# A weight gradient by seven products: two sums in other places, three stores in halves, and a new hand-written order

## The chip, the cores and the metric

The kernel runs on one core of a Trainium2 chip, in one launch. TensorE (PE) multiplies into PSUM, which has eight banks of 128 x 512 float32; VectorE (DVE) and ScalarE (ACT) empty and fill the banks and do sums; GpSimd (POOL) here only issues the loads, SyncE (SP) and ACT issue a few loads and the stores. The engines run apart from each other and wait for each other's semaphores. The metric is the device time of one execution in microseconds, as the median of several runs.

## The reference

```python
def reference(input: np.ndarray, grad_output: np.ndarray) -> np.ndarray:
    grad_weight = np.einsum('bmk,bmn->kn', input, grad_output)
    return grad_weight.astype(np.float32)
```

`input` is 16 x 512 x 1024 and `grad_output` 16 x 512 x 768, both float32. The result is one 1024 x 768 matrix: a product with a contraction over all 8192 rows.

## The kernel before

The rows are loaded 256 at a time, in 32 loads of each input (`LOADS`). Seven of the loads ("s") are taken as two single tiles of 128 rows each, 14 in all, whose products are the plain ones. The other 25 ("P") are pairs of tiles, on which a scheme with seven products in place of eight is used. The loads convert float32 to bfloat16 on the way, except for the very first tiles, which are loaded as float32 and rounded by DVE and ACT (L201).

The output is cut into four quarters: A (left columns, first half of the rows), B (right, first), C (left, second) and D (right, second), each of four blocks of 128 x 384, q = 0 to 3. For pairs seven products are summed over all items: A, B and C go on in the sums of the quarters, and 1, 5, 6 and 7 have sums of their own (`macc`; `SLOT` says where). D gets only the plain products. That makes 14 x 4 x 4 + 25 x 7 x 4 = 924 matmuls of 384 columns. For products 5, 6 and 7 DVE forms sums of the operands: `sum_x` (L183, L185, L187) and `sum_g` (L193, L195, L197), three steps each for each pair.

All of a block's matmuls can't stay in one bank for the whole run: there are 32 sums and eight banks. So a block is opened on a bank, gets a few matmuls, and is closed; a running sum is kept in SBUF. There are two ways to go on with a sum:

- `fill` (L264): ACT copies the sum back into a bank, and the matmuls add to it; the close is then a copy out, by ACT (L321) or DVE (L323).
- fresh: the matmuls start the bank anew, and the close is an add on DVE (L325).

The order of all engines' work is written out by hand in `PLAN`, a string of tokens read from left to right, which engines then carry out in that order, each for itself: `A0@1.2` is two matmuls of block A0, opened on bank 1 (without `@`: on the bank that it has); `fA2@6` fills A2 into bank 6; `cA2` and `vA2` close it by ACT or by DVE; `g0.7`, `g1.7`, `g2.7` and `x...` are the operand sums of item 7; `r0` to `r4` are roundings of the first tiles. `fB2@1+2` fills a block in two parts, 256 columns in bank 1 and 128 in bank 2, and its matmuls are then done first for the one and then for the other.

A block's last close is always on DVE. It brings the shared sums in (`SHARED`, L310), and for product 5 makes two results:

```python
nc.vector.tensor_sub(out=dst, in0=b, in1=sum_of("6", q))                      # L306
nc.vector.tensor_sub(out=sum_of("6", q), in0=b, in1=sum_of("7", q))           # L307
```

B then adds the first of them (slot 5) and D the second (slot 6). L307 writes the slot that L306 reads, and in the built program it waits for L306 by DVE's own semaphore. After the final close of A, B, C and D the block is stored (L315), by SP, except for the part of 128 columns, which ACT stores. The stores take the eight semaphores of their kind in turn. In the built program the last but one, 128 columns on ACT's queue, has the fourth, and the 256 columns on SP's queue the fifth. At the very end SP waits for the eight of them one after the other, first to eighth, and then come the barriers of all engines.

The plan's last tokens are `52.4 vD3 vB0 C2.6 v52 fD2@0 fB2@1+2 D0.2 vC2 D2.2 B2.6 vD0 vD2 vB2`.

Of the kernel before, what the change touches and what calls it, by code (L numbers as in the profile page):

```python
# [9 lines left out]
P = 128  # L10
# [9 lines left out]


PLAN = (
    "A0@0.1 A2@1.1 A3@2.1 A1@3.1 vA2 C2@6.1 cA3 C3@7.1 C0@4.1 r0 cC2 C1@5.1 vC3 B0@1.1 B1@2.1 B2@6.1 cB0 "
    "r1 B3@7.1 r2 r3 vB1 D0@1.2 r4 A0.1 vB2 A1.1 cB3 D1@2.2 vD0 D2@6.2 cD1 D3@7.2 vD2 C0.1 C1.1 cD3 "
    "C2@1.1 C3@2.1 B0@6.2 vC2 B1@7.2 vC3 fA2@1 A0.1 A1.1 vB0 C0.1 A3@2.2 vB1 A2.2 B2@6.2 vA3 cA2 B3@7.3 "
    "vB2 C1.2 vB3 C3@2.2 C2@1.2 vC3 D0@6.2 D1@7.2 vC2 D2@2.2 vD0 fD3@1 A0.2 vD1 C0.2 fA3@6 D3.3 vD2 "
    "B2@7.2 cD3 A3.2 vB2 B1@2.2 cA3 A2@1.3 vB1 fB3@6 B0@7.3 vA2 fD2@2 B3.2 vB0 C3@1.2 cB3 D2.2 vC3 D1@7.2 "
    "cD2 C2@6.2 vD1 fD0@1 A1.3 vC2 A3@2.1 D0.2 vA3 B1@7.1 D3@6.1 cD0 C1.2 vB1 fB2@2 A0.1 C0.3 vD3 B2.3 "
    "C2@1.2 cB2 D2@7.2 vC2 A2@6.2 fC3@2 A1.2 vD2 fD1@1 C3.2 vA2 D0@7.2 cC3 D1.2 vD0 D3@6.2 cD1 A3@2.2 vD3 "
    "B1@7.2 B0@1.2 vA3 fB3@6 A0.2 vB1 C1.2 vB0 B3.4 fA2@7 A3@2.2 vB3 B0@1.2 A2.2 vA3 fB1@6 A0.2 vB0 cA2 "  # L30
    "A1.2 fB2@2 B1.2 C2@1.2 cB1 C3@7.2 vC2 C0.2 fD1@6 C1.2 vC3 fD2@1 B2.2 fD3@7 D1.4 vB2 D2.4 cD1 D3.4 "
    "cD2 D0@2.1 g0.6 D0.3 cD3 B3@6.1 g1.6 fA2@7 B3.1 vD0 C3@1.2 A2.1 g2.6 A2.1 fA3@2 A0.2 vB3 cA2 A1.2 "
    "vC3 A3.2 fC2@6 x0.6 A3.1 fB0@7 C0.3 cA3 C2.1 x1.6 C2.2 C1.1 x2.6 C1.2 cC2 B1@1.1 g0.7 B1.2 fA2@6 "
    "B0.3 vB1 B2@2.2 g1.7 cB0 B2.1 A2.1 g2.7 fC3@1 A0.1 10@7.1 vB2 A1.1 cA2 C3.1 v10 13@2.2 cC3 x0.7 "
    "12@6.2 c13 11@7.2 v12 73@1.2 c11 52@2.1 x1.7 52.1 c73 70@6.2 x2.7 53@7.2 c52 g0.8 C0.1 c70 50@1.2 "
    "v53 51@2.2 c50 g1.8 60@6.2 v51 fB3@7 A0.1 61@1.2 c60 g2.8 A1.1 B3.2 v61 C2@6.2 x0.8 cB3 C1.2 10@2.2 "
    "vC2 71@1.2 x1.8 71.1 72@7.3 v10 c71 63@6.1 x2.8 63.2 c72 g0.9 62@1.3 fB0@2 v63 C3@7.2 c62 B0.1 g1.9 "
    "B0.1 fA3@6 A1.1 vC3 C0.1 A0.1 fA2@1 g2.9 A3.2 x0.9 cB0 A3.1 A2.3 cA3 13@7.1 x1.9 f11@2 13.1 C1.1 vA2 "
    "A0.1 fB1@6 C0.1 x2.9 11.2 fB2@1 B1.3 v13 c11 g0.10 B2.3 f52@7 vB1 73@2.2 cB2 52.1 g1.10 52.1 f12@6 "
    "A1.1 v73 70@1.2 c52 12.1 g2.10 12.1 f53@2 x0.10 12.1 50@7.2 c12 53.3 v70 f61@6 C1.1 x1.10 51@1.3 c53 "  # L40
    "v50 61.2 x2.10 f60@2 61.1 C2@7.1 g0.11 C2.1 c61 60.3 v51 fB3@6 A0.1 g1.11 C0.1 62@1.2 c60 vC2 B3.2 "
    "g2.11 B3.1 C3@2.3 v62 cB3 x0.11 10@7.3 f71@1 A1.2 f72@6 vC3 71.2 x1.11 71.1 72.3 v10 c71 63@2.1 "
    "x2.11 63.2 f13@7 g0.12 B0@1.3 c72 v63 13.2 73@6.1 g1.12 fA2@2 73.1 vB0 C0.1 A0.1 c13 C1.1 g2.12 A2.2 "
    "f11@1 x0.12 A2.1 A3@7.3 cA2 v73 11.2 f52@2 x1.12 11.1 70@6.3 vA3 c11 52.1 x2.12 52.2 f50@1 g0.13 "
    "51@7.2 c52 50.3 v70 12@2.1 g1.13 12.1 c50 B1@6.3 v51 fB2@1 C1.1 g2.13 C2@7.3 v12 C0.1 x0.13 C0.1 "
    "f53@2 A1.2 B2.3 vB1 A0.1 x1.13 A0.1 cB2 53.3 vC2 f62@1 60@6.1 g0.14 60.2 c53 62.1 x2.13 62.2 g1.14 "
    "61@7.3 v60 c62 B3@2.1 g2.14 B3.2 f10@1 v61 C3@6.3 x0.14 f71@7 10.3 vB3 C1.2 c10 71.1 x1.14 71.2 vC3 "
    "73@1.3 c71 x2.14 13@2.2 f72@6 g0.15 13.1 A1.1 fB0@7 C0.1 v13 72.3 g1.15 B0.3 v73 c72 63@2.1 g2.15 "
    "63.2 cB0 x0.15 A0.2 f11@6 A2@7.3 v63 f12@1 11.2 x1.15 11.1 12.3 vA2 c11 51@2.1 x2.15 fA3@7 51.2 "
    "g0.16 B1@6.3 c12 v51 A3.2 f52@1 g1.16 A3.1 C1.1 vB1 50@2.3 cA3 g2.16 52.3 f70@6 v50 fC2@7 A1.2 x0.16 "  # L50
    "70.3 c52 C2.1 x1.16 C2.2 c70 B2@2.1 x2.16 B2.2 cC2 g0.17 53@1.3 f60@7 vB2 62@6.3 g1.17 60.3 f61@2 "
    "v53 C0.1 g2.17 C0.1 c60 61.3 v62 B3@7.1 x0.17 B3.2 f13@6 C3@1.3 c61 vB3 13.2 f72@2 x1.17 13.1 C1.2 "
    "vC3 c13 72.2 x2.17 72.1 f63@6 73@1.1 g0.18 73.2 c72 10@7.1 g1.18 10.2 fB0@2 v73 63.3 g2.18 B0.3 v10 "
    "c63 A0.1 x0.18 A0.2 cB0 C0.2 f51@7 71@1.1 x1.18 71.3 fA3@2 x2.18 A1.2 v71 A3.3 g0.19 51.3 cA3 52@6.1 "
    "g1.19 52.2 c51 g2.19 B1@1.3 v52 f11@7 A2@2.3 vB1 f12@6 11.2 x0.19 f50@1 11.2 12.4 vA2 c11 x1.19 50.3 "
    "c12 x2.19 50.1 70@2.1 fC2@6 g0.20 70.3 c50 B2@7.1 g1.20 B2.3 v70 f53@1 C2.1 g2.20 C2.2 vB2 53.3 cC2 "
    "60@2.3 v53 f62@6 C1.2 x0.20 fB3@1 C1.1 61@7.3 v60 62.2 x1.20 62.1 B3.3 v61 c62 C3@2.1 g0.21 C3.2 cB3 "
    "13@6.1 x2.20 f10@7 13.2 g1.21 A0.2 f72@1 vC3 10.3 g2.21 72.3 v13 c10 A1.1 x0.21 A1.2 c72 C0.3 fA3@1 "
    "x1.21 73@2.3 x2.21 73.1 63@6.1 g0.22 63.3 v73 B0@7.4 v63 fA2@2 A3.2 g1.22 A3.1 vB0 A2.3 cA3 g2.22 "
    "51@6.3 f71@7 vA2 C1.2 f52@1 x0.22 A0.2 f12@2 52.4 v51 x1.22 71.4 fB1@6 v52 B1.1 g0.23 B1.2 c71 12.1 "  # L60
    "x2.22 12.2 cB1 g1.23 C2@1.3 c12 g2.23 50@7.3 vC2 f13@2 11@6.2 x0.23 fB2@1 11.2 13.3 v50 B2.3 v11 c13 "
    "53@7.1 x1.23 53.2 cB2 g0.24 53.1 f60@6 70@2.4 v53 f62@1 60.1 x2.23 60.2 f61@7 g1.24 60.1 62.4 v70 "
    "c60 g2.24 C0.3 fB3@6 v62 61.2 x0.24 fC3@1 61.2 10@2.4 v61 C3.1 x1.24 f72@7 C3.3 v10 B3.2 g0.25 cC3 "
    "B3.2 fA2@2 x2.24 72.2 g1.25 72.2 cB3 A2.1 g2.25 A2.2 c72 A1.3 cA2 x0.25 A1.1 C1.3 f63@2 x1.25 A0.3 "
    "x2.25 A3@1.4 g0.26 73@6.4 vA3 51@7.2 g1.26 51.2 fB0@1 v73 63.2 g2.26 63.2 v51 B1@6.3 c63 x0.26 B1.1 "
    "fC2@7 B0.4 vB1 C2.2 x1.26 cB0 C2.2 12@2.1 x2.26 12.2 cC2 g0.27 12.1 50@6.4 f71@7 v12 52@1.1 g1.27 "
    "fB2@2 52.3 v50 71.1 g2.27 71.3 f13@6 v52 B2.2 x0.27 c71 B2.2 C0.2 cB2 x1.27 C0.1 13.2 x2.27 13.2 "
    "11@1.2 c13 g0.28 11.2 53@7.4 f60@6 v11 70@2.1 g1.28 f61@1 70.3 v53 60.1 g2.28 60.3 v70 61.2 x0.28 "
    "c60 61.2 fB3@2 A0.3 v61 A1.2 x1.28 fC3@1 A1.1 C1.2 x2.28 C1.1 62@7.1 g0.29 62.3 g1.29 62.1 B3.5 v62 "
    "g2.29 A2@6.4 vB3 C3.1 x0.29 C3.4 vA2 10@7.2 cC3 x1.29 10.3 f63@6 x2.29 72@2.5 v10 g0.30 A3@1.4 f10@7 "  # L70
    "v72 63.4 vA3 f11@2 C0.1 g1.30 C0.1 c63 13@1.1 g2.30 13.2 x0.30 f12@6 11.3 v13 12.3 c11 x1.30 12.1 "
    "f61@1 10.1 A0.2 v12 f63@2 A1.2 x2.30 c10 61.3 f62@6 63.1 C1.2 v61 f60@7 62.2 v63 fA2@1 C0.1 60.3 v62 "
    "fA3@2 A2.4 v60 f71@6 A0.2 f72@7 vA2 A1.2 71.4 vA0 f70@1 vA1 f73@0 A3.3 v71 f51@3 C1.2 vA3 73.5 vC1 "
    "51.5 v73 f53@2 fC3@5 70.3 v51 fD1@0 53.3 fB1@6 C3.3 v70 f50@3 C0.2 v53 fD3@1 B1.7 vC3 fB3@2 50.4 vC0 "
    "vB1 B3.4 v50 fD0@4 72.1 fB0@5 D1.2 D3.2 vB3 B0.7 v72 f52@3 fC2@6 vD1 52.4 vD3 vB0 C2.6 v52 fD2@0 "
    "fB2@1+2 D0.2 vC2 D2.2 B2.6 vD0 vD2 vB2 "
).split()


# [2 lines left out]
SUMS_HELD = 10  # L82

MERGED = 3


@with_exitstack
def kernel(
# [6 lines left out]
    nc = tc.nc  # L95
# [3 lines left out]
    B, M, K = input.shape  # L99
# [9 lines left out]
    OUT = out.rearrange("(ks p) n -> p ks n", p=P)  # L109
# [36 lines left out]
    for u, kind in enumerate(LOADS):  # L146
# [3 lines left out]
        if u >= MERGED:  # L150
            rows = slice(2 * u * P, 2 * (u + 1) * P)
# [93 lines left out]
    def sum_of(p, q):  # L245
        if p in SLOT:
            return macc[:, SLOT[p], q, :]
        row = q if p in "AB" else Q + q
        return acc[:, row, LEFT if p in "AC" else RIGHT]

    SHARED = {"A": "1", "B": "5", "C": "7", "D": "6", "6": "1", "7": "6"}

    done = {(p, q): 0 for p in streams for q in range(Q)}
    fresh = {(p, q): True for p in streams for q in range(Q)}
    closed = set()
    opened = {}
    used = {7}

    def bank(b):
# [34 lines left out]
    def close(engine, p, q):  # L296
# [3 lines left out]
        if final and p not in "1":  # L300
            assert engine == "v" and (carried or fresh[p, q])
            for tile_, c0, c1 in parts:
                b = tile_[:, 0 : c1 - c0]
                if p == "5":
                    assert ("6", q) in closed and ("7", q) in closed
                    nc.vector.tensor_sub(out=dst, in0=b, in1=sum_of("6", q))  # L306
                    nc.vector.tensor_sub(out=sum_of("6", q), in0=b, in1=sum_of("7", q))  # L307
                else:
                    assert (SHARED[p], q) in closed and (p != "D" or ("5", q) in closed)
                    nc.vector.tensor_add(out=dst[:, c0:c1], in0=b, in1=sum_of(SHARED[p], q)[:, c0:c1])  # L310
                if p in "ABCD":
                    row = q if p in "AB" else Q + q
                    at = (0 if p in "AC" else NH) + c0
                    store = nc.scalar if c1 - c0 == 128 else nc.sync
                    store.dma_start(out=OUT[:, row, at : at + c1 - c0], in_=dst[:, c0:c1])  # L315
        else:
            ((b, _, _),) = parts
            b = b[:, 0:NH]
# [60 lines left out]
```

## Time and profile before

| what | value |
|---|---|
| median of 3 runs | 162.83 us (162.75 to 162.85) |
| the profiled execution, its own time | 162.72 us |
| its span, first to last instruction | 160.95 us |
| granted TensorE clock | 1.00 |
| fills, ACT 128x384 (L273) | 124, 0.48 us each |
| copies out, ACT (L321) | 105, 0.48 us each |
| final closes, DVE, 128x384 (L310) | 0.55 us each |
| final closes, DVE, 128x256 and 128x128 | 0.41 and 0.28 us |
| landing of a store after its issue | 1.9 to 2.2 us |

The busy time of an engine is the union of its instructions; instructions of DVE and ACT that follow each other without a wait overlap a little, so starts can be closer together than one instruction is long. Matmuls overlap too: one of 384 columns is shown as 0.33 us long and the next starts 0.16 us after it.

### The profile page before, as it was taken

Reading aid. Unit: us, or ns where it says so; the run is one execution under the profiler, and the core shown is the slowest. Engines: PE = TensorE matmul, PEld = TensorE weight load, DVE = VectorE, ACT = ScalarE, POOL = GpSimd, SP = SyncE. Lnnn points to the kernel's source line nnn. Section 1 sums busy time; section 2 is a strip of 40 time slices with the busy share of each in tenths; the row PEclk is TensorE's granted clock in tenths of the full one; section 3 lists DMA queues with packets and bytes.
Section 4 is the critical chain, followed back from the end, with each engine's and each line's share of the span. In section 5 each row is a group of like instructions: output and inputs, shape, how many; then the busy total and the mean of one; then the engine's idle time right before and its main releaser. Section 6 shows DMA issues by size and latency. Waiting matters only on the chain.

```text
span 161.0 us, 2767 instructions
## 1 busy us (share of the span) xinstructions
PE 155.2 (96%) x936; PEld 92.1 (57%) x936; DVE 144.2 (90%) x328; ACT 107.1 (67%) x237; POOL 35.7 (22%) x71
## 2 busy tenths in 40 slices
PE   8899999999999999999999999999999999999990
PEld 3356566555666566556665566556655665556650
DVE  0789978688999999999999999999999899989991
ACT  3653765887879878677977777577736632797530
POOL 7445222122221222222212222212222100000000
PEclk9999999999999999999999999999999999999999
DMA  4999999999999999999999999999999999916455
GB/s 173 300 207 212 212 215 213 213 212 215 215 211 215 213 210 215 212 212 212 213 216 212 213 213 212 213 215 213 212 213 213 215 211 212 210 29 244 147 196 196
DMA packets 12685, 33.40 MB, mean 207 GB/s; under 512 B 1408, under 2 KB 4480, under 8 KB 12672
## 3 DMA queue, kind: packets, MB, share of 16 engines
q0 software_dynamic: 9648, 28.64, 90.2%
q1 hardware_dynamic: 2592, 3.47, 6.1%
q10 hardware_dynamic: 432, 1.11, 1.8%
q8 instruction: 7, 0.11, 0.3%
q14 instruction: 6, 0.05, 0.1%
HBM read 58.72 MB, written 3.15 MB: 384 GB/s over the span
## 4 chain that ended last, share of the span: by engine, by line
PE 91%; DMA 3%; DVE 1%; ACT 1%; DVEq 0%; issue 0%; SPq 0%; ACTq 0%
PE bank L286 91%; DMA gf<-in_grad_output_dram 3%; DVE acc L325 1%; ACT acc L321 1%; DVEq L374 0%; ACT bank L273 0%; SPq L127 0%; DVE gp L201 0%; DVE gp L197 0%; DVE ge L195 0%; DVE acc L310 0%; ACTq L321 0%
## 5 line engine op out<-in xcount | busy, mean ns | idle before, releaser
L286 PE MATMUL bank<-gp,xp 128*128 128x384 bf16 (+1 forms) x630 | 110.6, 324 | 0.6 <-ACT xp L201 0.3
L286 PEld LDWEIGHTS <-xp 128*128 128x128 bf16 x630 | 61.3, 98 | 42.4 <-DVE xp L201 1.6
L286 PE MATMUL bank<-ge,xe 128*128 128x384 bf16 x300 | 57.1, 326 | 0.0
L286 PEld LDWEIGHTS <-xe 128*128 128x128 bf16 x300 | 29.3, 98 | 19.5 <-DVE xe L183 0.2
L273 ACT COPY bank<-acc 128x384 f32<-128x384 f32 (+2 forms) x63 | 29.3, 478 | 12.1 <-DVE acc L325 5.6
L325 DVE TENSOR_TENSOR acc<-bank,acc 128x384 f32<-128x384 f32 x64 | 33.4, 551 | 3.7 <-PE bank L286 2.7
L321 ACT COPY acc<-bank 128x384 f32<-128x384 f32 x50 | 23.9, 479 | 15.5 <-PE bank L286 14.9
L273 ACT COPY bank<-macc 128x384 f32<-128x384 f32 x63 | 29.8, 485 | 5.9 <-DVE macc L325 2.6
L321 ACT COPY macc<-bank 128x384 f32<-128x384 f32 x55 | 26.0, 479 | 11.0 <-PE bank L286 10.7
L325 DVE TENSOR_TENSOR macc<-bank,macc 128x384 f32<-128x384 f32 x50 | 27.3, 550 | 0.1
L153 POOL DMA_DIRECT2D xp<-in_input_dram x29 | 15.3, 527 | 50.4 <-DMA xp<-in_input_dram 25.6
L152 POOL DMA_DIRECT2D gp<-in_grad_output_dram x29 | 15.3, 528 | 37.0 <-PE bank L286 14.6
L183 DVE TENSOR_TENSOR xe<-xp 128x1024 bf16<-128x1024 bf16 x25 | 17.0, 681 | 0.1
L193 DVE TENSOR_TENSOR ge<-gp 128x768 bf16<-128x768 bf16 x25 | 13.7, 550 | 1.2 <-DMA gp<-in_grad_output_dram 1.2
L187 DVE TENSOR_TENSOR xp<-xp,xe 128x512 bf16<-128x512 bf16 x25 | 10.5, 418 | 0.4
L185 DVE TENSOR_TENSOR xe<-xe,xp 128x512 bf16<-128x512 bf16 x25 | 10.4, 416 | 0.2
L195 DVE TENSOR_TENSOR ge<-gp,ge 128x384 bf16<-128x384 bf16 x25 | 8.7, 349 | 0.2
L197 DVE TENSOR_TENSOR gp<-ge,gp 128x384 bf16<-128x384 bf16 x25 | 8.7, 349 | 0.2
L310 DVE TENSOR_TENSOR acc<-bank,macc 128x384 f32<-128x384 f32 (+2 forms) x17 | 8.0, 523 | 0.1
L323 DVE COPY acc<-bank 128x384 f32<-128x384 f32 x12 | 6.5, 552 | 1.3 <-PE bank L286 1.3
L323 DVE COPY macc<-bank 128x384 f32<-128x384 f32 x12 | 6.6, 552 | 0.5 <-ACT acc L321 0.3
L201 DVE CAST gp<-gf 128x192 bf16<-128x192 f32 (+1 forms) x2 | 0.6, 309 | 4.5 <-DMA gf<-in_grad_output_dram 4.4
(17 smaller groups left out, 24.3 us busy)
## 6 DMA issues: line engine op xcount, KB each, us to landing
xp<-in_input_dram POOLq DMA_DIRECT2D x29, 512.0 KB, 16.9
gp<-in_grad_output_dram POOLq DMA_DIRECT2D x29, 384.0 KB, 16.8
out_dram<-acc SPq DMA_DIRECT2D x15, 192.0 KB, 1.9
xf<-in_input_dram ACTq DMA_DIRECT2D x2, 512.0 KB, 4.9
xp<-in_input_dram POOLq DMA_DIRECT2D x4, 256.0 KB, 8.5
gp<-in_grad_output_dram POOLq DMA_DIRECT2D x5, 192.0 KB, 7.6
gf<-in_grad_output_dram SPq DMA_DIRECT2D x2, 192.0 KB, 4.4
out_dram<-acc SPq DMA_DIRECT2D x1, 128.0 KB, 2.0
```

The source lines that it names most:

```text
L152: nc.gpsimd.dma_start(out=gp, in_=G[rows, :].rearrange("(p m) n -> p m n", m=2))
L153: nc.gpsimd.dma_start(out=xp, in_=X[rows, :].rearrange("(p m) k -> p m k", m=2))
L183: nc.vector.tensor_sub(out=xe[:, 0:2, :], in0=x[:, 1::-1, :], in1=x[:, 3::-2, :])
L185: nc.vector.tensor_sub(out=xe[:, 2, :], in0=xe[:, 0, :], in1=x[:, 0, :])
L187: nc.vector.tensor_add(out=x[:, 1, :], in0=x[:, 2, :], in1=xe[:, 2, :])
L193: nc.vector.tensor_add(out=ge[:, 0:2, :], in0=g[:, 0:2, :], in1=g[:, 1::2, :])
L195: nc.vector.tensor_add(out=ge[:, 2, :], in0=g[:, 3, :], in1=ge[:, 0, :])
L273: nc.scalar.copy(out=tile_[:, 0 : c1 - c0], in_=src[:, c0:c1])
L286: nc.tensor.matmul(tile_[:, 0 : c1 - c0], stat, mov[:, c0:c1], start=first and j == 0, stop=True, skip_group_check=True,)
L321: nc.scalar.copy(out=dst, in_=b)
L323: nc.vector.tensor_copy(out=dst, in_=b)
L325: nc.vector.tensor_add(out=dst, in0=b, in1=dst)
```

## The change

`PLAN` is a new string: 1069 tokens for 1004. The matmuls are the same in number of columns. By kind:

| tokens | before | after |
|---|---|---|
| fills | 125 | 163 |
| closes on ACT | 105 | 112 |
| closes on DVE | 166 | 160 |
| operand sums | 150 | 150 |
| blocks opened without a fill | 146 | 109 |

The other edits:

```diff
-    SHARED = {"A": "1", "B": "5", "C": "7", "D": "6", "6": "1", "7": "6"}
+    SHARED = {"A": "1", "B": "6", "C": "7", "D": "5", "6": "1", "7": "6"}
...
+HALVED = 3
...
                 if p == "5":
                     assert ("6", q) in closed and ("7", q) in closed
-                    nc.vector.tensor_sub(out=dst, in0=b, in1=sum_of("6", q))
-                    nc.vector.tensor_sub(out=sum_of("6", q), in0=b, in1=sum_of("7", q))
+                    nc.vector.tensor_sub(out=sum_of("6", q), in0=b, in1=sum_of("6", q))
+                    nc.vector.tensor_sub(out=dst, in0=b, in1=sum_of("7", q))
...
-                    store = nc.scalar if c1 - c0 == 128 else nc.sync
-                    store.dma_start(out=OUT[:, row, at : at + c1 - c0], in_=dst[:, c0:c1])
+                    store = nc.scalar if c1 - c0 == 256 else nc.sync
+                    halves = [slice(0, P)]
+                    if len(stored) < 2 * HALVED:
+                        halves = [slice(0, P // 2), slice(P // 2, P)]
+                    for rows in halves:
+                        stored.append(rows)
+                        store.dma_start(out=OUT[rows, row, at : at + c1 - c0], in_=dst[rows, c0:c1])
```

The first sum of product 5 is now made in place, in slot 6, and the second goes to slot 5; B reads slot 6 and D slot 5. In the built program the second sum has no wait for the first. The first three stores are issued as two of 64 rows each, so that there are 20 stores in place of 17; in the built program the last two have the seventh semaphore (256 columns, now on ACT's queue) and the eighth (128 columns, now on SP's).

The plan's tokens that the prediction speaks of, at the start, at the first pairs' products, and from 50.3 to the end:

```diff
-A0@0.1 A2@1.1 A3@2.1 A1@3.1 vA2 C2@6.1 cA3 C3@7.1 C0@4.1 r0 cC2 C1@5.1 vC3 B0@1.1 B1@2.1 B2@6.1 cB0 r1 B3@7.1 r2 r3 vB1 D0@1.2
+A0@0.1 A3@1.1 A2@2.1 C3@7.1 vA3 C2@6.1 cA2 C0@4.1 C1@5.1 r0 cC3 A1@3.1 vC2 B2@1.1 D2@2.1 D1@7.1 cB2 r1 D3@6.1 r2 r3 vD2 D0@1.2
...
-B2@2.2 g1.7 cB0 B2.1 A2.1 g2.7 fC3@1 A0.1 10@7.1 vB2 A1.1 cA2 C3.1 v10 13@2.2 cC3 x0.7
+B2@2.2 g0.7 cB3 B2.1 C3.3 fB0@7 vB2 C0.1 fA2@1 A1.1 g1.7 73@2.1 vC3 B0.1 A2.1 c73 A0.1 vB0 11@6.1 cA2 13@2.1 g2.7 13.1
...
-51.5 v73 f53@2 fC3@5 70.3 v51 fD1@0 53.3 fB1@6 C3.3 v70 f50@3 C0.2 v53 fD3@1 B1.7 vC3 fB3@2 50.4 vC0 vB1 B3.4 v50 fD0@4 72.1 fB0@5 D1.2 D3.2 vB3 B0.7 v72 f52@3 fC2@6 vD1 52.4 vD3 vB0 C2.6 v52 fD2@0 fB2@1+2 D0.2 vC2 D2.2 B2.6 vD0 vD2 vB2
+50.3 vA3 C2.3 v50 fB0@0 52.2 fD0@3 B0.7 vC2 v52 fB2@1 51.2 fD2@5 B2.6 vB0 v51 fD1@6 73.1 D0.2 fB1@0 D2.2 vB2 B1.7 v73 f53@4 fC3@1 vD0 53.4 vD2 vB1 C3.5 v53 fD3@2 D1.2 fB3@0+7 D3.2 vC3 B3.7 vD1 vD3 vB3
```

## The prediction

> **What bounds the kernel now.** I read the page's busy shares first, then the chain of waits, then a table by stage, then the last microseconds on each engine and queue.
>
> ```profile
> span 161.0 us, 2767 instructions
> ...
> PE 155.2 (96%) x936; PEld 92.1 (57%) x936; DVE 144.2 (90%) x328; ACT 107.1 (67%) x237; POOL 35.7 (22%) x71
> ...
> PE 91%; DMA 3%; DVE 1%; ACT 1%; DVEq 0%; issue 0%; SPq 0%; ACTq 0%
> ```
>
> TensorE sets the time. The chain in order of time shows the only place in mid-run where something else is on it, and the end:
>
> ```profile
> 36.98 0.49 ACT bank L273
> 37.48 0.54 DVE acc L325
> 38.02 0.28 DVE ge L195
> 38.30 0.02 issue
> 38.32 0.36 DVE gp L197
> 38.67 0.48 DVE acc L325
> 39.15 0.04 issue
> 39.20 117.37 PE bank L286 x726
> ```
>
> The last 12 of those 726 matmuls are six pairs of 256 and 128 columns, so 720 full ones take 117.37 us: 0.163 us each, stalls included. Laying that pitch against the recorded starts gives all stalls of PE after its first real matmul: 0.29 and 0.24 us at 6.8 and 7.7 us, 0.05 at 11.1, 0.07 at 18.0, 0.22 at 39.2, 0.08 in three pieces, 0.10 at 138.5 (a load that had just landed): 1.05 us. That is all that a better order can win inside the matmul stream.
>
> By stage (columns: engine busy us and instructions, clock, DMA share, GB/s) and then the last adds and stores:
>
> ```profile
> 40.00:100.00 60.00, 60.00 (x371) 36.05 (x369) 59.36 (x142) 47.23 (x107) 14.61 (x28) 1.00 1.07 213
> ...
> 148.20:156.60 8.40, 8.35 (x58) 5.21 (x55) 8.30 (x19) 4.26 (x10) 0.00 (x0) 1.00 0.46 164
> 156.60:157.70 1.10, 0.00 (x0) 0.00 (x0) 1.03 (x4) 0.00 (x0) 0.00 (x0) 1.00 0.60 214
> 157.70:161.00 3.30, 0.00 (x0) 0.00 (x0) 0.00 (x0) 0.00 (x0) 0.00 (x0) 1.00 0.49 167
> ```
>
> ```profile
> 153.18 1.47 DVE L310 TENSOR_TENSOR acc<-bank,macc 128x384 f32<-128x384 f32 x3
> 154.57 0.55 DVE L306 TENSOR_TENSOR macc<-bank,macc 128x384 f32<-128x384 f32 x1
> 155.15 0.56 DVE L307 TENSOR_TENSOR macc<-bank,macc 128x384 f32<-128x384 f32 x1
> 155.63 2.00 DVE L310 TENSOR_TENSOR acc<-bank,macc 128x384 f32<-128x384 f32 x5
> ```
>
> The last matmul ends at 156.55 (call it E), but VectorE is never idle from 148.2 on and finishes 1.08 us later, at 157.63. So the tail belongs to VectorE's queue. After it come one store and the closing waits:
>
> ```profile
> 157.66 0.36 ACTq L315 DMA_DIRECT2D out_dram<-acc  x1
> ...
> L374 SPq EVENT_SEMAPHORE  x5: 28/28/28, 159.8 to 160.1; - x5
> ```
>
> **The working, part by part.** *The two sums of product 5.* At L306 to L307 the starts are 155.15 - 154.57 = 0.58 us apart, because L307 overwrites what L306 reads only after waiting for L306's write. Adds without such a wait stand at (1.47 - 0.55) / 2 = 0.46 us; the trace's own starts give 0.4645. After the change the second sum waits for nothing of the first: 0.115 us less, four times. Each counts only where VectorE is behind.
>
> *The order of the tail.* I lay VectorE's tail out anew from E backwards. After 50.3 the new plan still has 3+2+7+2+6+1+2+2+7+4+5+2+2+7 = 52 matmuls: 8.48 us at 0.163. So v50 can start at E - 8.45 (0.03 from a matmul's end to the engine, as in the chain at 7.11). Behind it stand 18 full adds (v50, C2, v52, B0, v51, B2, 73, D0, D2, B1, v53, C3, D1, D3, where each 5x counts two), and the matmuls of each end before its turn. 18 x 0.4645 = 8.36: the 256-column add starts at E - 0.09, the 128-column one 0.33 later (now 157.02 and 157.35) and lasts 0.28. VectorE ends at E + 0.52 instead of E + 1.08: 0.56 us won, 0.46 of it from the four waits, 0.10 from the order. By the same count the fills of these blocks (0.48 us each, after the add that frees the bank) end at least 0.4 us ahead of their matmuls, so PE isn't held.
>
> The Trainium skill speaks against this part ("VectorE: DVE Perf Modes", The DRAIN you can't avoid): an operation cannot start until the pipe of the one before is empty, and a semaphore between them adds nothing. By that rule the four waits are worth 0 and the sum below is 0.46 us higher, 162.4; the rows above (0.58 against 0.46) contradict it.
>
> *The last store and its semaphore.* Now the last store to land is the 128 columns on ACT's queue with the fourth semaphore: issued 157.66, 2.13 us to landing (the line's landings are 1.9 to 2.2). SP's closing waits go through the eight semaphores in order; that for the fourth is met at 159.81 and the four behind it, long fulfilled, still take their turn at 159.87, 159.93, 159.99 and 160.05. After the change the last store has the eighth: 160.05 - 159.81 = 0.24 us gone. Everything after the last wait (0.90 us to 160.95) stays. ACT takes the 256 columns and SP the last 128. SP is free in time: its D3 store issues at about E + 0.01, takes 0.34 and 0.09 more of waiting, so it is ready at E + 0.44 and the 128 columns come at E + 0.52. No gain or loss there; bounds from the landings are ±0.15.
>
> *Three stores in two halves.* Three more issues on SP of 0.33 to 0.61 us each, about 12 us before E. VectorE and PE wait for no store; the next stores in SP's queue come late by at most 3 x 0.61 = 1.8 us, and the six sums of v50, v52 and v51, which store nothing (2.8 us), take that up. Cost 0; were that cover gone, what is left of the 1.8 us would be added to the last store. The load queues are not passed; ACT issues no other store.
>
> *The matmul stream.* Work is the same (the last block is 14 short matmuls for 7, instead of 12 for 6). The start keeps its two stalls: the first block after the second half of g0 waits for that rounding as before, and D0 still takes a bank three matmuls after ACT begins to empty it. At 39.2 the cause was an add that stood behind L195 and L197 for a bank which was needed five matmuls later. Same stage, new order: B2's add goes ahead of L195's counterpart and frees its bank just in time (0.33 + 0.04 + 0.56 + 0.05 = 0.98 us, six pitches are 0.98); C3's add then stands behind L195's and costs about 0.07. So 0.15 less. The last two loads are needed three matmuls (0.49 us) later than now, so the 0.10 at 138.5 goes. Against that I put 0.10 of new small stalls: many banks are reused at the same shortest distance (five matmuls) elsewhere. Net -0.15; bounds -0.5 (all but the start, and about what the last landing at 142.8 allows) and, upwards, open.
>
> *ScalarE and VectorE in mid-run.* 38 more fills and 7 more copies out, 6 fewer closes on VectorE. VectorE loses 6 x 0.46 = 2.8 us of queue where it is 99% busy (59.36 of 60.00), but PE has no stall of weight there, so I credit 0. ACT gains 45 copies: at its queued pitches (0.38 after a copy out, 0.42 after a fill) some 18 us more, on 107. In the busiest hundred matmuls (16.3 us) it has 35 copies, 14.0 us at 0.40. It fits, and costs 0 while it does.
>
> *Sum.* -0.56 - 0.24 - 0.15 = -0.95 us on the profiled execution of 162.72 (span 160.95 and 1.77 around it): 161.77. That execution lies 0.11 below the median of 162.83, so the forecast is 161.9 (161.88).
>
> **The rivals.** *The stream gives the tail's win back.* A new order of over a thousand steps meets waits that the old one avoided; 0.24 us per bank taken back after three matmuls, as at 7.7, is the price of one. With 0.5 to 1.2 us of new stalls: 162.4 to 163.1. For it: several banks at the shortest distance, one ACT copy at distance four near 39 us. Against it: the stream before has only 0.5 us of such stalls outside the start.
>
> *ScalarE becomes the bound (slower).* Place: matmuls 200 to 500, where copies are 33 to 35 a hundred. If copies don't overlap there (0.48 each, as the copies out often stand now), 35 take 16.8 us against 16.3 of matmuls. It decides as soon as a fill comes later than the 0.3 us that a bank freed ten matmuls ahead leaves; 38 more fills at 0.05 us each make 1.9 us: 161.9 + 1.9 = 163.8. Against it: the trace's stage of 47.23 us for 107 copies kept PE at 60.00 of 60.00.
>
> *The second sum gains nothing.* The wait is gone from the program, but if the pipe keeps them apart, the tail ends 0.46 later: 162.3.
>
> **How the numbers follow.** About 0.2% (0.33 us) is what a measurement of this kernel can tell from no change: 162.50 to 163.16. Forecast (161.4 to 162.2) 0.60; second sum gains nothing 0.12, still faster; stream gives it back 0.16, of which 0.04 stay below 162.50 and 0.12 are the same; ScalarE 0.12, slower. Faster 0.76, same 0.12, slower 0.12. The range goes from 161.4 (0.35 more won in the stream and 0.1 at the landing) to 162.7, which leaves out most of ScalarE's case and part of the second: about 0.2.
>
> **What would show it.** Starts of the two 5-sums 0.46 us apart; VectorE ending about 0.5 us after the last matmul; the last landing followed by one closing wait, not five; PE's stalls adding to 0.8 to 1.0 us, with two of 0.29 and 0.24 at the start. Wrong it would be if the last matmul ends later than 157.2, or if PE's chain holds ACT fills in mid-run.

## The result and the profile after

The changed kernel takes 162.23 us (median of 6 runs, 162.05 to 162.46); the kernel before, on the same chip, takes 162.84 (6 runs, 162.75 to 163.03). The ratio is 0.9961, with a 95% interval of 0.9949 to 0.9974: 0.6 us faster. The forecast was 161.9, inside a range of 161.4 to 162.7. So the sign and the range held, and about a third of the forecast gain of 0.95 us did not come.

In the changed kernel the code stands 6 to 13 lines lower: the sums of product 5 are L314 and L315 (L306, L307 before), the last closes L318 (L310), fills L281 (L273), copies out by ACT L334 (L321), the other closes by DVE L336 and L338 (L323, L325), matmuls L294 (L286), stores L328 (L315), the closing waits L387 (L374).

The page of the changed kernel, whose profiled execution took 162.41 us: span, busy time of each engine, shares of the chain by engine.

```profile
span 160.6 us, 2815 instructions
...
PE 156.1 (97%) x937; PEld 92.4 (58%) x937; DVE 141.9 (88%) x322; ACT 124.2 (77%) x282; POOL 35.7 (22%) x71
...
PE 95%; DVE 2%; issue 1%; ACT 0%; DVEq 0%
```

Work went from VectorE (144.2 before) to ScalarE (107.1 before), as the plan's tokens say, and TensorE still sets the time. The chain of waits of the changed kernel in order of time (start, us, what):

```profile
7.39 0.49 ACT acc L334
7.88 0.04 issue
7.92 145.43 PE bank L294 x890
153.35 0.53 DVE acc L318 x2
```

The break near 39 us is gone from the chain: from 7.92 to 153.35 it is matmuls alone. That looks like a stream without stalls, and is not. The table by stage of the changed kernel (columns as before: PE, PEld, DVE, ACT, POOL busy, clock, DMA share, GB/s):

```profile
40.00:100.00 60.00, 60.00 (x369) 35.83 (x367) 57.80 (x136) 52.82 (x124) 14.36 (x28) 1.00 1.07 213
...
148.00:157.00 9.00, 8.99 (x63) 5.66 (x60) 9.00 (x21) 4.46 (x11) 0.00 (x0) 1.00 0.72 237
157.00:157.60 0.60, 0.00 (x0) 0.00 (x0) 0.60 (x3) 0.00 (x0) 0.00 (x0) 1.00 1.00 361
157.60:160.60 3.00, 0.00 (x0) 0.00 (x0) 0.00 (x0) 0.00 (x0) 0.00 (x0) 0.89 0.56 190
```

In 40 to 100 us PE is again shown busy 60.00 of 60.00, yet 369 matmuls stand there in place of 371. A matmul is shown 0.33 us long and the next one starts 0.1625 after it, so busy time has no hole until a stall is longer than 0.16. Stalls of this size are seen only in the distance between recorded starts. The last two rows are the new end: VectorE works 0.60 us past the last matmul (1.08 before), and 3.01 us of stores, waits and barriers follow (3.32 before).

### Where the time is

Every trace of this study splits in the same way. Let the ninth matmul of the real data be the anchor: it is the first that needs the second half of the first `grad_output` load (`r0`). Then the last matmul's end E is

    E = start of the ninth matmul + 149.26 to 149.27 us + stalls after 9 us

in all thirteen traces, whatever the order (the stalls are the recorded distances less 0.1625, for matmuls of 384 columns). Two more terms follow: VectorE's end after E, and the span's end after VectorE's.

| profiled execution | ninth matmul | stalls after 9 us | VectorE after E | end after VectorE | span |
|---|---|---|---|---|---|
| before | 6.78 | 0.51 | 1.08 | 3.32 | 160.95 |
| after | 7.03 | 0.69 | 0.60 | 3.01 | 160.61 |
| difference | +0.26 | +0.18 | -0.48 | -0.30 | -0.34 |

The first column is not the change's: the matmuls up to the ninth wait for the same loads and for the same clock, and over the traces it lies anywhere from 6.60 to 7.25, for the same kernel too (6.91 in another trace of the changed kernel). The seven traces of the old order average 7.01, the six of the new order 6.98. The other three make +0.18 - 0.48 - 0.30 = -0.60, which is what the medians show (-0.61).

VectorE's timeline at the end of the changed kernel (start, us, engine, line, operation):

```profile
147.14 1.56 DVE L318 TENSOR_TENSOR acc<-bank,macc 128x384 f32<-128x384 f32 x3
148.62 0.55 DVE L314 TENSOR_TENSOR macc<-bank,macc 128x384 f32<-128x384 f32 x1
149.09 0.55 DVE L315 TENSOR_TENSOR macc<-bank,macc 128x384 f32<-128x384 f32 x1
...
154.66 0.55 DVE L314 TENSOR_TENSOR macc<-bank,macc 128x384 f32<-128x384 f32 x1
155.13 0.55 DVE L315 TENSOR_TENSOR macc<-bank,macc 128x384 f32<-128x384 f32 x1
155.59 2.00 DVE L318 TENSOR_TENSOR acc<-bank,macc 128x384 f32<-128x384 f32 x5
```

The two sums of product 5 now start 0.47 us apart (0.58 before). And SP's closing waits from 159.6 to 159.97 us (count, ns each, first and last start), where the last store lands at 159.69:

```profile
L387 SPq EVENT_SEMAPHORE  x1: 28/28/28, 159.7 to 159.7; - x1
```

One wait behind the last landing, where there were five.

### The profile page after: what moved, and what is told of

Read it like the earlier page. It is cut to its first block, busy times and chain, and to the rows that moved or that the text cites. A ratio compares the mean times of both kernels' runs of the same rounds, so it can differ in the third digit from the quotient of the medians.

```text
span 160.6 us, 2815 instructions
## 1 busy us (share of the span) xinstructions
PE 156.1 (97%) x937; PEld 92.4 (58%) x937; DVE 141.9 (88%) x322; ACT 124.2 (77%) x282; POOL 35.7 (22%) x71
## 4 chain that ended last, share of the span: by engine, by line
PE 95%; DVE 2%; issue 1%; ACT 0%; DVEq 0%
PE bank L294 92%; PE bank L142 3%; DVE acc L318 1%; ACT acc L334 0%; DVE macc L314 0%; DVEq L387 0%; DVE macc L315 0%
## 5 line engine op out<-in xcount | busy, mean ns | idle before, releaser
L294 PE MATMUL bank<-gp,xp 128*128 128x384 bf16 (+2 forms) x631 | 111.8, 325 | 0.1
L294 PEld LDWEIGHTS <-xp 128*128 128x128 bf16 x631 | 61.6, 98 | 42.4 <-DVE xp L208 1.6
L294 PE MATMUL bank<-ge,xe 128*128 128x384 bf16 x300 | 58.0, 326 | 0.0
L281 ACT COPY bank<-acc 128x384 f32<-128x384 f32 (+1 forms) x82 | 38.0, 480 | 7.8 <-DVE acc L318 2.0
L281 ACT COPY bank<-macc 128x384 f32<-128x384 f32 x82 | 38.6, 485 | 6.1 <-DVE macc L336 2.7
L294 PEld LDWEIGHTS <-xe 128*128 128x128 bf16 x300 | 29.3, 98 | 19.6
L334 ACT COPY macc<-bank 128x384 f32<-128x384 f32 x61 | 28.6, 480 | 6.0 <-PE bank L294 4.6
L334 ACT COPY acc<-bank 128x384 f32<-128x384 f32 x51 | 24.1, 479 | 7.9 <-PE bank L294 7.1
L338 DVE TENSOR_TENSOR acc<-bank,acc 128x384 f32<-128x384 f32 x45 | 24.3, 553 | 2.0 <-PE bank L294 1.3
L336 DVE COPY acc<-bank 128x384 f32<-128x384 f32 x30 | 16.2, 554 | 3.7 <-PE bank L294 3.1
L338 DVE TENSOR_TENSOR macc<-bank,macc 128x384 f32<-128x384 f32 x32 | 17.7, 554 | 1.6 <-PE bank L294 1.5
L190 DVE TENSOR_TENSOR xe<-xp 128x1024 bf16<-128x1024 bf16 x25 | 17.1, 684 | 0.0
L336 DVE COPY macc<-bank 128x384 f32<-128x384 f32 x25 | 13.7, 555 | 1.7 <-PE bank L294 1.2
L318 DVE TENSOR_TENSOR acc<-bank,macc 128x384 f32<-128x384 f32 (+2 forms) x17 | 8.2, 524 | 0.0
```

Source lines behind the costliest of these rows:

```text
L190: nc.vector.tensor_sub(out=xe[:, 0:2, :], in0=x[:, 1::-1, :], in1=x[:, 3::-2, :])
L281: nc.scalar.copy(out=tile_[:, 0 : c1 - c0], in_=src[:, c0:c1])
L294: nc.tensor.matmul(tile_[:, 0 : c1 - c0], stat, mov[:, c0:c1], start=first and j == 0, stop=True, skip_group_check=True,)
L334: nc.scalar.copy(out=dst, in_=b)
L336: nc.vector.tensor_copy(out=dst, in_=b)
L338: nc.vector.tensor_add(out=dst, in0=b, in1=dst)
```

## The experiments

All ran beside the kernel before, whose medians were 162.80 (21 runs, 162.67 to 162.98) for the first four, 162.80 (15 runs, 162.68 to 162.95) for the next four and 162.81 (11 runs, 162.74 to 163.34) for the last three. The two theories were: (a) the small edits give all of the gain and more, and the new order gives part of it back through new stalls; (b) the order gives part of the gain, and the small edits less than was worked out.

### The stores alone, in the old order

```diff
+HALVED = 3
...
-                    store = nc.scalar if c1 - c0 == 128 else nc.sync
+                    store = nc.scalar if c1 - c0 == 256 else nc.sync
...
+                    for rows in halves:
+                        stored.append(rows)
+                        store.dma_start(out=OUT[rows, row, at : at + c1 - c0], in_=dst[rows, c0:c1])
```

> The kernel before with the store edits alone (first three stores in halves, 256 columns on ACT's queue, the last 128 on SP's with the eighth semaphore). Theory: VectorE still ends about 1.08 us after the last matmul, but only one closing wait follows the last landing: 0.25 to 0.30 us less than before, 162.5 to 162.6. Rival (closing waits are hidden behind the barriers): no change, 162.8.

162.52 us (11 runs, 162.41 to 162.81), ratio 0.9985 (0.9976 to 0.9994): -0.28. In its trace the end after VectorE is 3.00 (3.32 before), VectorE after E 1.09 (1.08). The gain lies where it was put: 0.24 of it are the four waits that no longer stand behind the last landing, and the way from VectorE's end to the last landing's wait is 0.06 shorter.

### Product 5's sums alone, in the old order

```diff
-    SHARED = {"A": "1", "B": "5", "C": "7", "D": "6", "6": "1", "7": "6"}
+    SHARED = {"A": "1", "B": "6", "C": "7", "D": "5", "6": "1", "7": "6"}
...
-                    nc.vector.tensor_sub(out=dst, in0=b, in1=sum_of("6", q))
-                    nc.vector.tensor_sub(out=sum_of("6", q), in0=b, in1=sum_of("7", q))
+                    nc.vector.tensor_sub(out=sum_of("6", q), in0=b, in1=sum_of("6", q))
+                    nc.vector.tensor_sub(out=dst, in0=b, in1=sum_of("7", q))
```

> The kernel before with product 5's sums placed anew, alone. Theory: the second sum starts 0.465 us after the first and not 0.58; three of the four stand in the stretch in which VectorE is never idle up to its end, so the end comes 3 x 0.115 = 0.35 us earlier: 162.5. Rival (the pipe keeps the two apart, with or without the wait): no change, 162.8.

162.24 us (5 runs, 162.09 to 162.48), ratio 0.9966 (0.9952 to 0.9979): -0.56. VectorE's timeline at the end of this kernel:

```profile
154.34 0.55 DVE L306 TENSOR_TENSOR macc<-bank,macc 128x384 f32<-128x384 f32 x1
154.81 0.55 DVE L307 TENSOR_TENSOR macc<-bank,macc 128x384 f32<-128x384 f32 x1
155.27 2.00 DVE L310 TENSOR_TENSOR acc<-bank,macc 128x384 f32<-128x384 f32 x5
```

From L306 to L307 it takes 0.47, from L307 to the next last close 0.46; before it was 0.58 and 0.48. VectorE ends 0.51 after E in place of 1.08. All four waits count, not three as expected, because VectorE has no idle time from the first of these sums (147.2 us) to its end. In the recorded starts of the two traces each wait costs 0.115 between the two sums and 0.010 more at the next close, four times 0.125 = 0.50. The other 0.07 comes once, at the first sum of the first pair:

```profile
147.22 0.56 DVE L306 TENSOR_TENSOR macc<-bank,macc 128x384 f32<-128x384 f32 x1 [0.26 <-PE bank L286]
```

```profile
147.36 0.56 DVE L306 TENSOR_TENSOR macc<-bank,macc 128x384 f32<-128x384 f32 x1 [0.18 <-PE bank L286]
```

Before (first line) it starts 0.11 after the end of the matmul that it waits for (147.11), in this kernel (second line) 0.04 after it (147.33). In the records before it waits first for TensorE and then for ScalarE; here it has the one wait, for TensorE.

### Both small edits, in the old order

```diff
+HALVED = 3
...
-    SHARED = {"A": "1", "B": "5", "C": "7", "D": "6", "6": "1", "7": "6"}
+    SHARED = {"A": "1", "B": "6", "C": "7", "D": "5", "6": "1", "7": "6"}
...
-                    store = nc.scalar if c1 - c0 == 128 else nc.sync
+                    store = nc.scalar if c1 - c0 == 256 else nc.sync
```

> The kernel before with both small edits and its own old order. If the two add up: 0.60 to 0.65 us less, 162.2, that is, as fast as the changed kernel, and the new order is then worth nothing. If the new order is worth the 0.10 to 0.25 that the prediction gave it, this one stays at 162.35 or above.

161.89 us (5 runs, 161.82 to 162.31), ratio 0.9947 (0.9935 to 0.9960): -0.91, against -0.28 - 0.56 = -0.84 for the two alone. They add up, since the one shortens VectorE's way and the other what comes after. This is also less than the changed kernel's 162.23, from another series: without the new order the kernel looks faster than with it. The last two runs compare the two side by side.

### The changed kernel with the old sums

```diff
-    SHARED = {"A": "1", "B": "6", "C": "7", "D": "5", "6": "1", "7": "6"}
+    SHARED = {"A": "1", "B": "5", "C": "7", "D": "6", "6": "1", "7": "6"}
...
-                    nc.vector.tensor_sub(out=sum_of("6", q), in0=b, in1=sum_of("6", q))
-                    nc.vector.tensor_sub(out=dst, in0=b, in1=sum_of("7", q))
+                    nc.vector.tensor_sub(out=dst, in0=b, in1=sum_of("6", q))
+                    nc.vector.tensor_sub(out=sum_of("6", q), in0=b, in1=sum_of("7", q))
```

> The changed kernel with the old places of product 5's sums. Theory: all four pairs stand in the last busy stretch, each 0.115 us longer: 0.46 us more than the changed kernel, 162.7. Rival (the wait costs nothing): as the changed kernel, 162.2.

162.78 us (11 runs, 162.44 to 163.10), ratio 0.9998 (0.9989 to 1.0007): no different from before, and 0.55 slower than the changed kernel. VectorE's timeline at its end:

```profile
155.25 0.55 DVE L314 TENSOR_TENSOR macc<-bank,macc 128x384 f32<-128x384 f32 x1
155.83 0.56 DVE L315 TENSOR_TENSOR macc<-bank,macc 128x384 f32<-128x384 f32 x1
156.30 2.01 DVE L318 TENSOR_TENSOR acc<-bank,macc 128x384 f32<-128x384 f32 x5
```

The 0.58 is back, and VectorE ends 1.11 after E, 0.51 later than in the changed kernel: four times 0.127. So the sums are worth about the same in both orders (0.56 and 0.55 by the medians, 0.57 and 0.51 by the traces). This kernel is the new order with the stores' edit, and the first experiment the old order with it: 162.78 against 162.52, the new order 0.26 slower.

### The changed kernel without the halves

```diff
-HALVED = 3
+HALVED = 0
```

> The changed kernel with no store in halves: 17 stores, the last two (256 columns on ACT's queue, 128 on SP's) with the fourth and fifth semaphore. Theory: three fulfilled closing waits of 0.06 us follow the last landing: 0.18 us more than the changed kernel, 162.4. Rival (the win of the store edits comes from handing the last two stores to the other queues): 162.2.

162.36 us (11 runs, 162.18 to 162.74), ratio 0.9978 (0.9969 to 0.9987), 0.13 above the changed kernel with overlapping runs. With 17 stores the last one has the fifth semaphore. SP's closing waits of this kernel from 159.7 to 160.04 us:

```profile
L387 SPq EVENT_SEMAPHORE  x4: 27/28/28, 159.8 to 160.0; - x4
```

Four waits from the last landing on, at 0.06 us each three more than in the changed kernel: 0.18. The end after VectorE is 3.20 in place of 3.01, so the closing waits explain all of it, and the halves cost nothing that shows: stalls (0.69) and VectorE's tail (0.60) are the same with and without them.

### Three late fills taken out

The distances between matmul starts show where the stalls after 9 us are (us; pieces above 0.014):

    before         11.1 .05   18.0 .07   39.2 .22   51.9 .03   53.4 .02   106.1 .02   138.5 .10
    after          11.7 .03   16.0 .07   19.7 .02   21.1 .03   38.6 .03    39.4 .09    41.2 .02
                   43.5 .07   51.8 .16   57.7 .08   81.4 .15
    three fresh    11.3 .03   15.5 .07   19.3 .02   20.6 .03   38.2 .03    38.9 .08    40.7 .02
                   43.1 .06   53.3 .05   54.4 .36

Those at 51.8, 57.7 and 81.4 in the changed kernel wait for a fill of ScalarE. ScalarE's timeline at the last of them, and TensorE's:

```profile
80.50 0.48 ACT L334 COPY macc<-bank 128x384 f32<-128x384 f32 x1 [0.29 <-ACT acc L334]
80.88 0.49 ACT L281 COPY bank<-macc 128x384 f32<-128x384 f32 x1
81.29 0.48 ACT L281 COPY bank<-acc 128x384 f32<-128x384 f32 x1
```

```profile
80.45 0.65 PE L294 MATMUL bank<-ge,xe 128*128 128x384 bf16 x3
80.94 1.12 PE L294 MATMUL bank<-gp,xp 128*128 128x384 bf16 x5
```

The fill of 80.88 ends at 81.37, and a matmul starts 0.05 after it, at 81.42. Five matmuls in a row take 4 x 0.1625 + 0.33 = 0.98, but the second line says 1.12: that is the stall, and no idle time is shown with it.

The three fills are late in three ways. Here the fill comes behind a copy out that starts 0.29 after the copy before it has ended (80.21), although its matmuls have ended at 80.13; why it starts so late isn't shown. At 57.7 it comes behind two queued copies, on a bank that VectorE's close gave back only at 57.08; and at 51.8 it comes behind the copy out of its own bank:

```profile
56.38 0.48 ACT L281 COPY bank<-acc 128x384 f32<-128x384 f32 x1 [0.52 <-DVE macc L338]
56.80 0.47 ACT L334 COPY macc<-bank 128x384 f32<-128x384 f32 x1
57.17 0.90 ACT L281 COPY bank<-macc 128x384 f32<-128x384 f32 x2
```

```profile
50.74 0.48 ACT L334 COPY macc<-bank 128x384 f32<-128x384 f32 x1
51.25 0.48 ACT L281 COPY bank<-acc 128x384 f32<-128x384 f32 x1
```

All three were made fresh blocks, which wait for no ScalarE; `B3` and `11` are then closed by an add on VectorE.

```diff
-72.2 fB3@6 g1.10 63@7.2 c72 vB2 B3.2 g2.10 B3.1 11@2.3 v63 cB3
+72.2 g1.10 63@7.2 c72 vB2 B3@6.2 g2.10 B3.1 11@2.3 v63 vB3
...
-C2.3 f73@6 A0.1 vA3 f53@7 73.2
+C2.3 A0.1 vA3 f53@7 73@6.2
...
-x2.16 f11@1 60.2 g0.17 A1.1 fA2@2 C1.1 11.3 v60 f51@7 A2.1 g1.17 A2.2 c11
+x2.16 60.2 g0.17 A1.1 fA2@2 C1.1 11@1.3 v60 f51@7 A2.1 g1.17 A2.2 v11
```

> The changed kernel with three of its blocks (B3 near 51.8 us, product 7's third sum near 57.7, product 1's second near 81.4) opened fresh and closed by an add on VectorE (the second is closed by VectorE either way), and not filled by ScalarE. Theory (the new order loses because ScalarE's fills come late for TensorE): the stalls of 0.16, 0.08 and 0.15 us at these places go, 0.3 to 0.4 us less, 161.85 to 161.95. Rival (the order loses elsewhere, or VectorE's added work gives it back): 162.2.

162.20 us (5 runs, 161.98 to 162.63), ratio 0.9965 (0.9953 to 0.9978): no gain. The three stalls are gone, but the sum is 0.72 for 0.69. TensorE's timeline of this kernel:

```profile
52.81 1.35 PE L294 MATMUL bank<-gp,xp 128*128 128x384 bf16 x7
54.36 0.48 PE L294 MATMUL bank<-ge,xe 128*128 128x384 bf16 x2 [0.20 <-ACT bank L281]
```

`vB3` stands longer in VectorE's queue than `cB3` did in ScalarE's; the closes behind it come later, a fill waits for one of them until 53.82 and the matmuls for that fill until 54.36. The stall went from one engine's queue to the other's.

### An operand sum behind the close that the old order held up

The old order's stall at 39.2 comes from the close of `B2` behind two operand sums. Here the second of them is put behind it, in the kernel with both small edits.

```diff
-B2.1 A2.1 g2.7 fC3@1 A0.1 10@7.1 vB2 A1.1 cA2
+B2.1 A2.1 fC3@1 A0.1 10@7.1 vB2 g2.7 A1.1 cA2
```

> The kernel before with both small edits and one token moved: the third sum of g for the item near 38 us stands behind the add of B2, not ahead of it. Theory: the stall of 0.22 us near 39.3, the largest left in mid-run, goes: 161.7 against 161.9. Rival (the time comes back in the next steps): 161.9.

162.00 us (5 runs, 161.95 to 162.05), ratio 0.9952 (0.9939 to 0.9964), not to be told from 161.89. The 0.22 is gone from its place and comes back in three: 0.08 at 39.97, 0.12 at 40.57, 0.04 at 47.9. So moving this one step only changed which of the steps waits. That VectorE's work there is late as a whole, whatever the order, is argued from this one trial.

### A part of product 5 on GpSimd

```diff
+                    nc.gpsimd.tensor_sub(out=dst, in0=sum_of("6", q), in1=sum_of("7", q))
                     nc.vector.tensor_sub(out=sum_of("6", q), in0=b, in1=sum_of("6", q))
-                    nc.vector.tensor_sub(out=dst, in0=b, in1=sum_of("7", q))
+                    nc.gpsimd.tensor_add(out=dst, in0=sum_of("6", q), in1=dst)
```

> As the one before, and product 5's second result made by GpSimd from the first: it forms the difference of the sums of 6 and 7 ahead of time and adds it after VectorE's first sum, so that VectorE has four adds of 0.465 us less in the tail. Theory (VectorE's queue is what is left between the last matmul and the last store): it ends 0.3 us after the last matmul and not 0.5: 161.5. Rival (GpSimd's add takes so long that the last D waits for it, or its use of SBUF slows VectorE): 161.7 or above.

165.10 us (4 runs, 165.00 to 165.32), ratio 1.0144 (1.0130 to 1.0158): 3.1 us slower than the kernel that it was made from. GpSimd's timeline:

```profile
147.85 1.00 POOL L311 TENSOR_TENSOR macc<-macc 128x384 f32<-128x384 f32 x1 [1.28 <-DVE macc L310]
148.81 0.99 POOL L309 TENSOR_TENSOR macc<-macc 128x384 f32<-128x384 f32 x1
150.47 1.00 POOL L311 TENSOR_TENSOR macc<-macc 128x384 f32<-128x384 f32 x1 [0.67 <-DVE macc L310]
```

and what VectorE waited for, in us in total, times, longest:

```profile
DVE macc L310 <- POOL macc L309: 2.3, 2, 1.6
```

One such operation takes 1.00 us on GpSimd, against 0.55 on VectorE, and in its queue a block's subtraction (L309) stands behind the addition of the block before (L311), so that VectorE waits for it. VectorE ends 0.99 after E (0.51 without GpSimd), and TensorE's stalls grow from 0.45 to 0.92, 0.45 of them at 150.96, for a fill behind such a wait. The largest loss comes after all work: the end after VectorE is 5.22 us in place of 3.01. SP's last signal to the barrier is at 160.10 and GpSimd answers it at 162.48, 2.4 us later, where the kernel that it was made from shows 0.02. GpSimd's closing instructions (count, ns shortest, median and longest):

```profile
L383 POOLq DRAIN  x3: 45/93/6594, 155.8 to 162.9; - x3
```

The longest one is the first: from 155.84 GpSimd stands in this drain until 162.44, 5.6 us past the end of its last addition (156.88). Why it lasts so long isn't shown.

### Two late fills taken out, and the two orders side by side

```diff
-C2.3 f73@6 A0.1 vA3 f53@7 73.2
+C2.3 A0.1 vA3 f53@7 73@6.2
...
-x2.16 f11@1 60.2 g0.17 A1.1 fA2@2 C1.1 11.3 v60 f51@7 A2.1 g1.17 A2.2 c11
+x2.16 60.2 g0.17 A1.1 fA2@2 C1.1 11@1.3 v60 f51@7 A2.1 g1.17 A2.2 v11
```

> The changed kernel with only two of the three late fills made fresh (73 at 57.7 us, 11 at 81.4 us; the first already closed on VectorE, the second's close goes from ScalarE to VectorE). The fill of B3 at 51.8 us stays, so that the place where the last trial lost 0.36 us is left alone. If such stalls simply add up at the end: 0.08 + 0.15 = 0.23 us of stall go and nothing new comes: stalls after 9 us 0.46 in place of 0.69, median 162.0. If VectorE's longer queue gives it back in another place: a new stall of 0.1 to 0.4 us behind 81 us and 162.2 or more.

162.16 us (6 runs, 161.79 to 162.40), ratio 0.9954 (0.9940 to 0.9967). In the trace it went as the first expectation said: stalls after 9 us 0.47 for 0.70 in the changed kernel beside it, and no new one. The median, 0.08 below that kernel's, is too close to say that the 0.23 arrived.

> The old order with both small edits once more, beside the changed kernel on one chip. If the new order costs time by itself: 161.9 here and 0.2 to 0.4 us more for the changed kernel. If the difference seen so far came from when the full clock was granted in those runs: both within 0.1 us of each other.

> The changed kernel as it is, beside the old order with both small edits. If the new order costs time by itself: 162.2, 0.2 to 0.4 us above the run before it. If not: within 0.1 us of it.

The old order with both small edits: 162.07 us (6 runs, 161.87 to 162.22), ratio 0.9948 (0.9936 to 0.9960). The changed kernel: 162.24 (6 runs, 162.05 to 162.60), ratio 0.9964 (0.9951 to 0.9977). That is 0.17 apart, less than either case named: the difference of 0.34 seen first was partly chance. Over all runs of both series the medians are 161.97 (11 runs) and 162.23 (12 runs). The traces say what the order itself costs, free of the start: stalls 0.69 and 0.70 against 0.46 and 0.40, VectorE after E 0.60 against 0.51, together 0.32 to 0.38. In sum: the new order costs 0.2 to 0.4 us; that it costs something is shown by the two pairs of kernels and by every trace, its size no better than that.

## Why the prediction was right, and where it was wrong

Its sum had three terms; the comparison of the two traces, less the start, has the same three:

| term | predicted | measured, after less before |
|---|---|---|
| VectorE's tail after E | -0.56 | -0.48 |
| last store and closing waits | -0.24 | -0.30 |
| matmul stream | -0.15 | +0.18 |
| sum | -0.95 | -0.60 |

**The two sums.** Right in place and about right in size: 0.46 was worked out, and taking the edit alone gives 0.56 in the old order and 0.55 in the new. In the traces it is 0.46 to 0.47 between the sums in both, 0.04 because the close behind each second sum also starts 0.01 sooner, and in the old order alone 0.07 at the first pair's first sum. The rival that the second sum gains nothing is refuted. The Trainium skill ("VectorE: DVE Perf Modes", The DRAIN you can't avoid) says that a semaphore between two operations costs nothing extra; on this kernel it costs 0.115 us each time between the two (0.58 against 0.465 apart), and 0.125 with the close behind them. The same section also says that a following operation which is not held starts earlier, and that agrees: 0.465 apart at 0.547 long.

**The tail's order.** This 0.10 did not come; the new order's tail is 0.09 longer than the old one's with the same sums (0.60 against 0.51). The step that failed is "v50 can start at E - 8.45": it started at 148.62, E - 8.37, and the 0.08 is still there at the end. The tail was laid out from `v50` on, as if VectorE came to it free; but the close of A3 stands ahead of it, as the last of the three in the 147.14 line, and waits for that block's own last matmul. This shows in the same view from 148 on:

```profile
147.60 1.10 DVE L318 TENSOR_TENSOR acc<-bank,macc 128x384 f32<-128x384 f32 x2
```

Two queued closes would take 0.465 + 0.547 = 1.01, and this says 1.10. A3's last matmul ends at 148.04, its close starts at 148.15, 0.54 behind the close before it, and `v50` follows 0.475 later.

**The last store.** The four waits are 0.24 as worked out, the landing another 0.06, inside its bounds of 0.15. The halves cost nothing, as said; what they do is to give the last store the eighth semaphore, and without them 0.19 of it is lost.

**The matmul stream.** Here the forecast lost 0.33 of the missing 0.35. Two of its three pieces were right: 39.2 went from 0.22 to 0.09 (0.07 was forecast), and the 0.10 at 138.5 is gone, though in the old order too it came and went with the load's landing (0.10, 0.05, and below 0.014 in five traces). The third, "0.10 of new small stalls", measured 0.60 for 0.20: 0.40. Nearly all of that is three fills at 51.8, 57.7 and 81.4.

**ScalarE.** The load was right: 17.1 us more (124.2 - 107.1) where 18 were worked out. "It fits, and costs 0 while it does" was the error behind the third piece. A sum over a hundred matmuls says that the copies fit on the average; in three places a fill was still 0.08 to 0.16 late, behind the copies just ahead of it. The rival in which ScalarE becomes the bound named the right mechanism, fills that come late, at the wrong scale: 1.9 us against 0.39. The argument set against it, PE at 60.00 of 60.00 busy, is one that cannot speak on stalls below 0.16. The rival in which the stream gives the win back asked for 0.5 to 1.2 us of new stalls, and 0.40 came.

**The signs that were named.** 5-sums 0.46 apart: so. VectorE ending about 0.5 us after the last matmul: 0.60. One closing wait: so. Stalls of 0.8 to 1.0 in all, two of them 0.29 and 0.24 at the start: 0.69 after 9 us and 0.24 at the start, 0.93 in all, but that it fits is luck, since the 0.29 was covered by a slower clock in this trace. E before 157.2: 157.0. ACT fills in the chain of waits: none listed, though three held PE.

The version that beats both kernels is the old order with both small edits: 161.89 and 162.07 in its two series, against 162.23 and 162.24 for the changed kernel and 162.8 for the one before.

## What to carry to other kernels

Price a removed wait where its engine is behind, and count what runs after the last landing: about 0.13 us four times and 0.06 us four times gave 0.7 to 0.9 us in the old order, and a new order of a thousand steps cost 0.2 to 0.4. A full engine's average says nothing of single late steps: look for stalls in the distance between matmul starts, since busy time and the chain hide those below 0.16 us. And when the work of a late engine is moved to its neighbour, follow the neighbour's queue from that place on, because the stall moves with it.

## What the runs showed of the hardware

**The start moves by 0.65 us from run to run, by one late piece of one load or by the clock.** VectorE's timeline of the old order with both edits, second series, and of the changed kernel with three fresh blocks, at the rounding that the ninth matmul waits for:

```profile
6.84 0.36 DVE L202 CAST gp<-gf 128x384 bf16<-128x384 f32 x1 [0.57 <-DMA gf<-in_grad_output_dram]
```

```profile
6.19 0.35 DVE L208 CAST gp<-gf 128x384 bf16<-128x384 f32 x1
```

The load comes in sixteen pieces. In the first of these traces fifteen of them were there by 6.00 and the last at 6.82; in the second all by 5.95. The ninth matmul started at 7.25 and 6.60. In ten of the thirteen traces it starts 0.05 after the end of this rounding; in the other three, the changed kernel's first trace among them, it starts 0.16 after the eighth, which the slower clock of the next paragraph had made late. A spread of 0.65 is as large as the spread between the runs of one kernel (0.1 to 0.7 us), and the reason why differences of 0.2 us were read from the traces' other terms.

**The clock's edges lie on a grid.** In the changed kernel's trace the first matmuls of 384 columns start 0.30 to 0.32 apart until 6.1 us and 0.1625 after 6.38; in the trace of before the first eight are 0.16 to 0.17 apart from the start. The records put the full clock at 6.32 to 159.92 and at 4.33 to 161.34, that is 45 and 46 times 3.413 us; in all thirteen traces it lasts 45 or 46 times that, and it begins anywhere from 3.6 to 6.7. The Trainium skill ("TensorE: Matmul & The Clock Gate", What's actually happening) gives a window of 3413 ns that doesn't start with the kernel, and the records agree. Where the full clock began at 6.3 to 6.7 (three traces), the ninth matmul started at 7.03 to 7.23; where it began before 6, at 6.60 to 7.25, because the ninth waits for the load anyway. So much of a late edge is hidden here.

**A copy into a bank behind a copy out of the same bank waits for its end.** ScalarE's copies otherwise overlap by 0.1 us: above, the fill at 80.88 starts 0.38 after the copy out at 80.50. The fill of 51.25, into bank 6, follows the copy out of bank 6 of 50.74 and starts 0.51 after it, 0.03 after its end. It is 0.16 late for its matmul, though seven matmuls lie between the bank's last use and its next.

**A fulfilled closing wait costs 0.06 us, in order.** The four behind the last landing take 0.24 before, and three take 0.18 in the kernel without halves. By this, as an estimate, the place of the last store's semaphore among the eight counts up to 7 x 0.06 = 0.42 us.
